# Rotary tables of a two-layer decoder: 16 rows built with frequency and token group on the partitions, instead of 128 rows built by transposes

## The chip, the cores and the metric

The program runs on one core of a Trainium2 chip. The metric is the device time of one execution in microseconds, as the median of repeated runs. The core's engines work side by side, each in its own instruction order: TensorE (PE; its weight loads are shown apart as PEld), VectorE (DVE), ScalarE (ACT), GpSimd (POOL) and SyncE (SP, which here only issues transfers). Transfers are issued on the queues of SP, ACT and POOL.

## The reference, cut to what matters

Two layers follow each other over 1024 tokens of width 1024. A layer norms the stream, multiplies it with one combined weight matrix of 5376 columns, runs a sliding-window attention (8 query heads, 2 key/value heads of 64) and a gated linear recurrence on parts of the product, merges both under gates, and adds an output projection to the stream. All is float32. The change is to the tables of the rotary embedding, which turns the first 16 of the 64 entries of each query and key head:

```python
def partial_rope(x, positions):
    half = ROT_DIM // 2                                   # 8
    inv_freq = jnp.power(ROPE_THETA, -jnp.arange(half, dtype=jnp.float32) * (2.0 / ROT_DIM))
    ang = positions.astype(jnp.float32)[..., None] * inv_freq
    cos = jnp.cos(ang)[:, :, None, :]
    sin = jnp.sin(ang)[:, :, None, :]
    xr = x[..., :ROT_DIM].astype(jnp.float32)
    x1, x2 = xr[..., :half], xr[..., half:]
    rot = jnp.concatenate([x1 * cos - x2 * sin, x2 * cos + x1 * sin], axis=-1)
    return jnp.concatenate([rot.astype(x.dtype), x[..., ROT_DIM:]], axis=-1)

h = rms_norm(x, norm_w[layer])
proj = h @ w_in[layer]
(q, k, v, z_attn, q_h, f_h, i_h, g_h, gate_attn, gate_hgrn) = jnp.split(proj, split_points, axis=-1)
q = partial_rope(q.reshape(B, T, N_HEADS, HEAD_DIM), positions)
k = partial_rope(k.reshape(B, T, N_KV_HEADS, HEAD_DIM), positions)
...
x = x + merged @ w_out[layer]
```

So there are 8 frequencies times 1024 tokens = 8192 angles, and both layers use the same ones.

## The kernel before, in words

**Products.** Every float32 product is made of three matmuls on high and low halves (`hi` rounded, `lo = x - hi`; L394 to L396 in the pairs). The cast that makes `hi` is ScalarE's (L137), the difference `lo` VectorE's (L138).

**Pairs.** The combined projection of a layer is done as 15 pairs of 128-column weight chunks (`pair`, called in a loop over `m`). A pair uses a scheme with seven block products in place of eight: VectorE makes sums of quarter matrices of the weights (`ws`, L379 to L383), ScalarE and VectorE split them, and TensorE accumulates into two PSUM banks, `pb` and `pc` (further names are `th`, `tl` for the split sums of the activations and `hh`, `hl` for the split activations). A pair has 60 matmuls of 128x512, or 84 where the first product, `p1`, was not made ahead (in layer 0 from pair 12 on, in layer 1 from pair 11 on; there ScalarE copies `pb` out at L410 and L435 in place of VectorE's additions at L405, and the bank `pb` is then accumulated into again). Results go through buffers `pq`, an activation on ScalarE and a store.

**The tables.** `constants()` is a generator that the loop over pairs of layer 0 advances by one step behind each pair (two behind the first two). Its first step loads the small constants on SP's queue: `freq` [128, 8], `posi` [128, 8] (L508: token p of block b), sinks and norms. Later steps compute the angles (token on the partition; block and frequency along the row), bring them into the range of the sine and make `sins` and `nrn` (for 1 - 2 sin^2 of the half angle). The last four steps each fill a tile `tab` [128, 4x128] on GpSimd (L577), write the few columns that differ from 1 or 0 on VectorE, turn it by four TensorE transposes (L588) into a PSUM bank `tt`, copy it out on ScalarE (`tabo`, L590) and store it on ScalarE's queue into half of a DRAM table `tabs` [128, 1024] (L591). Table 0 holds cosines (1 in rows that are not turned), table 1 sines (0 there).

**The rotary work.** `rotary()` is a generator that `pair` advances, from pair 9 on (`TURN`), once for each result. GpSimd fills `other` with 0 (L715), loads the two tables into SBUF (`cosT`, `sinT`, L729), and for each of five tiles loads `y` (L719) and four pieces of 8 rows of it, exchanged, into `other` (L724). VectorE multiplies `y` by `cosT` (L734), `other` by `sinT` (L736) and adds them (L737); ScalarE casts the sum to `yh` (L742), VectorE makes the rest (L744), and GpSimd's queue stores both. Later GpSimd loads the turned tiles as `ks` and `qs` (L798), and the attention scores begin (L833).

**What sets the order.** Except for the first tokens, whose order is written by hand, a scheduler in the framework sets the order on each engine from the dependencies, the buffers and costs of its own. So a change at one place can move instructions at others. Each engine then works strictly in its order.

Of the kernel before, what the change touches and what calls it, by code (L numbers as in the profile page):

```python
# [24 lines left out]
HD = 64  # L25
# [16 lines left out]
def trunk_kernel(ctx, tc, x, positions, norm_w, w_in, attn_sinks, hgrn_norm_w, w_up_attn,  # L42
# [444 lines left out]
    tabs = [dp.tile([P, T], F32, name=f"tabs_{i}") for i in range(2)]  # L487
# [3 lines left out]
    def constants():  # L491
# [16 lines left out]
        nc.sync.dma_start(posi, positions.rearrange("o (b p) -> p (o b)", p=P))  # L508
# [35 lines left out]
        posf = cp.tile([P, NB], F32, name="posf")  # L544
        tc.keep_in_program_order(V.tensor_copy(posf, posi))
        ang = cp.tile([P, NB, HALF], F32, name="ang")
# [3 lines left out]
        nrn = cp.tile([P, NB, HALF], F32, name="nrn")  # L550
# [16 lines left out]
        sins = cp.tile([P, NB, HALF], F32, name="sins")  # L567
# [4 lines left out]
        for i in range(2):  # L572
            for g in range(2):
                yield
                b = slice(4 * g, 4 * g + 4)
                t = hp.tile([P, 4, P], F32, tag="po", name=f"tab_{i}_{g}")
                G.memset(t, 1.0 - i)  # L577
                for j in (0, HD):
                    if i:
                        V.tensor_scalar(out=t[:, :, j:j + HALF], in0=sins[:, b], scalar1=-1.0, scalar2=None, op0=ALU.mult)  # L580
                        V.tensor_copy(t[:, :, j + HALF:j + 2 * HALF], sins[:, b])
                    else:
                        for e in (j, j + HALF):
                            V.tensor_scalar(out=t[:, :, e:e + HALF], in0=nrn[:, b], scalar1=-2.0, scalar2=1.0,
                                            op0=ALU.mult, op1=ALU.add)
                tp = bank([P, 4, P], f"tt_{i}_{g}")
                for j in range(4):
                    PE.transpose(tp[:, j], t[:, j], ident)  # L588
# [18 lines left out]
    for L in range(DEPTH):  # L607
# [103 lines left out]
        def rotary():  # L711
            cosT, sinT = (slot([P, T], f"{n}T_{L}") for n in ("cos", "sin"))

# [14 lines left out]
            for t, d in zip((cosT, sinT), tabs):  # L728
                nc.gpsimd.dma_start(t, d)  # L729
# [697 lines left out]
def _constants():  # L1427
    p = np.arange(P)
    side = (p[:, None] <= p[None, :]).astype(np.float32)
    upper = (p[None, :] > p[:, None]).astype(np.int32)  # L1430
    s, t = (p % 32)[:, None], np.arange(32)[None, :]
    diag = (s == t).astype(np.float32)
    lev = [(s // (2 * h) == t // (2 * h)) & (s % (2 * h) < h) & (t % (2 * h) >= h) for h in (1, 2, 4, 8, 16)]
    lev = lev[:1] + [lev[1] & (s % 4 == i) for i in range(2)] + lev[2:4] + [lev[4] & (s // 8 % 2 == i) for i in range(2)]
    lev = np.stack(lev, axis=1).astype(np.int32)
    freq = np.power(np.float32(THETA), -np.arange(HALF, dtype=np.float32) * np.float32(2.0 / 16)).astype(np.float32)
    return {"c_ident": np.eye(P, dtype=np.float32), "c_side": side, "c_upper": upper, "c_diag": diag, "c_lev": lev,
            "c_freq": np.ascontiguousarray(np.broadcast_to(freq, (P, HALF)))}
# [27 lines left out]
```

## Time and profile before

| what | us |
|---|---|
| median of three runs | 1376.55 (1376.39 to 1377.52) |
| the profiled execution | 1377.78 |
| its span in the trace | 1376.0 |
| PE busy in it | 1359.2, x8252 |
| DVE busy | 993.3, x1616 |
| ACT busy | 704.1, x1390 |
| POOL busy | 116.6, x196 |

The span runs from the first to the last event of the profile on the core. Matmuls overlap, so that the duration in a row of TensorE is longer than the distance from one start to the next. In the rows of the timeline the first two columns are the start and the duration in us; behind them stand the engine (SPq and the like are the queues' issues), the line, the operation, what it writes and reads without buffer numbers, and shapes; at the end, in square brackets, how long the engine had been idle and what released it. In the rows of a windows view each engine has its busy us and, in brackets, its number of instructions.

### The profile page before, as it was taken

Reading aid. Unit: us, or ns where it says so; the run is one execution under the profiler, and the core shown is the slowest. Engines: PE = TensorE matmul, PEld = TensorE weight load, DVE = VectorE, ACT = ScalarE, POOL = GpSimd, SP = SyncE. Lnnn points to the kernel's source line nnn. Section 1 sums busy time; section 2 is a strip of 40 time slices with the busy share of each in tenths; the row PEclk is TensorE's granted clock in tenths of the full one; section 3 lists DMA queues with packets and bytes.
Section 4 is the critical chain, followed back from the end, with each engine's and each line's share of the span. In section 5 each row is a group of like instructions: output and inputs, shape, how many; then the busy total and the mean of one; then the engine's idle time right before and its main releaser. Section 6 shows DMA issues by size and latency. Waiting matters only on the chain.

```text
span 1376.0 us, 21533 instructions
## 1 busy us (share of the span) xinstructions
PE 1359.2 (99%) x8252; PEld 1129.6 (82%) x8252; DVE 993.3 (72%) x1616; ACT 704.1 (51%) x1390; POOL 116.6 (8%) x196
## 2 busy tenths in 40 slices
PE   9999999999999999999999999999999999999997
PEld 9888888888877888888888888888887788888885
DVE  5867668843646888599959666777356388867998
ACT  7754334443786665313566333344357766552254
POOL 2000012220000011000000001122100000100000
PEclk9999999999999999999999999999999999999998
DMA  8634477875225742390255345597923476429203
GB/s 274 204 114 145 140 223 212 263 266 208 92 93 190 266 158 78 141 403 38 77 176 188 122 143 178 169 255 223 315 96 100 133 236 207 147 88 404 90 0 123
DMA packets 204375, 240.06 MB, mean 174 GB/s; under 512 B 14288, under 2 KB 140880, under 8 KB 204272
## 3 DMA queue, kind: packets, MB, share of 16 engines
q1 hardware_dynamic: 156528, 145.08, 32.3%
q10 hardware_dynamic: 35088, 52.57, 10.5%
q0 software_dynamic: 12656, 41.04, 9.5%
q8 instruction: 65, 1.06, 0.3%
q14 instruction: 38, 0.31, 0.1%
HBM read 160.00 MB, written 78.64 MB: 173 GB/s over the span
## 4 chain that ended last, share of the span: by engine, by line
PE 89%; DVE 7%; DMA 2%; ACT 2%; issue 1%; DVEq 0%; ACTq 0%; SPq 0%
PE pb L394 6%; PE pb L396 6%; PE pb L395 6%; PE pc L394 4%; PE pc L396 4%; PE pc L395 4%; PE pg L233 3%; PE pg L234 3%; PE pg L235 3%; PE av L893 2%; PE pi L920 2%; PE pi L919 2%; PE pi L921 2%; PE pu_uh L968 2%; PE pj_qh L148 2%; PE pu_uh L970 2%
## 5 line engine op out<-in xcount | busy, mean ns | idle before, releaser
L137 ACT CAST whi_s<-ws 128x1024 fp32r<-128x1024 f32 x30 | 31.6, 1053 | 88.3 <-PE pc L396 88.3
L405 DVE TENSOR_TENSOR pq<-pc,pq 128x512 f32<-128x512 f32 x37 | 25.5, 690 | 61.4 <-PE pc L396 56.3
L631 ACT ACTIVATE pq<-pq 128x512 f32<-128x512 f32 x60 | 37.9, 631 | 44.4 <-DVE pq L405 42.9
L137 ACT CAST whi_o<-wo 128x1024 fp32r<-128x1024 f32 x20 | 21.1, 1054 | 77.0 <-PE pu_uh L970 35.5
L137 ACT CAST whi_t<-ws 128x1024 fp32r<-128x1024 f32 x30 | 31.6, 1055 | 41.9 <-PE pc L396 28.0
L968 PE MATMUL pu_ua<-wh_a,wlo_ua 128*128 128x512 f32 x128 | 52.0, 406 | 0.0
L857 ACT ACTIVATE pr<-pr,mx 128x128 f32<-128x128 f32 x128 | 49.6, 390 | 4.1 <-DVE mx L854 3.7
L1152 POOL COPY scT<-acc 32x256 f32<-32x256 f32 x32 | 26.3, 821 | 288.1 <-DVE acc L1149 169.5
L968 PE MATMUL pu_uh<-wh_b,wlo_uh 128*128 128x512 f32 x128 | 50.1, 391 | 0.5 <-DVE u L976 0.5
L970 PE MATMUL pu_ua<-wh_a,whi_ua 128*128 128x512 f32 x128 | 50.4, 394 | 0.0
L969 PE MATMUL pu_ua<-wl_a,whi_ua 128*128 128x512 f32 x128 | 49.9, 390 | 0.0
L969 PE MATMUL pu_uh<-wl_b,whi_uh 128*128 128x512 f32 x128 | 49.8, 389 | 0.0
L970 PE MATMUL pu_uh<-wh_b,whi_uh 128*128 128x512 f32 x128 | 49.8, 389 | 0.0
L394 PE MATMUL pb<-th,wl 128*128 128x512 f32 x120 | 47.1, 393 | 0.5 <-ACT pq L435 0.4
L394 PE MATMUL pb<-th,wlo_s 128*128 128x512 f32 x120 | 47.2, 394 | 0.2 <-DVE wlo_s L138 0.2
L233 PE MATMUL pg<-hh,wl_p 128*128 128x512 f32 (+1 forms) x128 | 46.9, 366 | 0.3 <-DVE wl_p L470 0.3
L394 PE MATMUL pc<-hh,wlo_t 128*128 128x512 f32 x120 | 46.9, 390 | 0.0
L395 PE MATMUL pb<-tl,whi_s 128*128 128x512 f32 x120 | 46.7, 390 | 0.0
L396 PE MATMUL pb<-th,whi_s 128*128 128x512 f32 x120 | 46.7, 389 | 0.0
L394 PE MATMUL pc<-th,wlo_s 128*128 128x512 f32 x120 | 46.7, 389 | 0.0
L395 PE MATMUL pb<-tl,wh 128*128 128x512 f32 x120 | 46.7, 389 | 0.0
L396 PE MATMUL pb<-th,wh 128*128 128x512 f32 x120 | 46.7, 389 | 0.0
(447 smaller groups left out, 4468.2 us busy)
## 6 DMA issues: line engine op xcount, KB each, us to landing
wr<-in_w_in_dram SPq DMA_DIRECT2D x72, 512.0 KB, 4.6
gd<-pq ACTq DMA_DIRECT2D x79, 256.0 KB, 3.0
fq<-fq ACTq DMA_DIRECT2D x48, 256.0 KB, 2.8
wr_p<-in_w_in_dram SPq DMA_DIRECT2D x23, 512.0 KB, 5.2
x<-in_x_dram SPq DMA_DIRECT2D x16, 512.0 KB, 7.5
qs<-qsd POOLq DMA_DIRECT2D x16, 512.0 KB, 7.6
u<-gd SPq DMA_DIRECT2D x16, 512.0 KB, 10.2
ga<-gd SPq DMA_DIRECT2D x16, 512.0 KB, 10.2
```

The costliest lines, as they stand in the source:

```text
L137: S.copy(hi, raw)
L233: PE.matmul(acc, lhsT=wl[:, k], rhs=h[:, t], start=k == ks[0][0], stop=False, skip_group_check=q > 0)
L234: PE.matmul(acc, lhsT=wh[:, k], rhs=l[:, t], start=False, stop=False, skip_group_check=q > 0)
L235: PE.matmul(acc, lhsT=wh[:, k], rhs=h[:, t], start=False, stop=k == ks[q][3], skip_group_check=q > 0)
L394: PE.matmul(acc, lhsT=wl[:, k], rhs=h, start=start and k == 0, stop=False, skip_group_check=not start)
L395: PE.matmul(acc, lhsT=wh[:, k], rhs=l, start=False, stop=False, skip_group_check=not start)
L396: PE.matmul(acc, lhsT=wh[:, k], rhs=h, start=False, stop=k == 3, skip_group_check=not start)
L631: S.activation(d, src, AF.Sigmoid if r < 2 * KT else AF.Silu)
L857: S.activation(pr[:, h], pr[:, h], AF.Exp, bias=mx[:, h:h + 1], accum_out=sm[:, h:h + 1])
L968: PE.matmul(acc, lhsT=w[1][:, k, c], rhs=hi[:, i], start=k == 0, stop=False)
L969: PE.matmul(acc, lhsT=w[0][:, k, c], rhs=lo[:, i], start=False, stop=False)
L970: PE.matmul(acc, lhsT=w[0][:, k, c], rhs=hi[:, i], start=False, stop=k == 3)
```

## The change

The angles are laid out anew: partition f*16 + g holds frequency f of the 64 tokens of group g, so that all tables are [128, 64] tiles. `posi` is loaded eight times, once for each frequency, into 16 partitions each. `freq` is a column [128, 1], and one operation makes all angles instead of eight. The DRAM tables keep only 2 x 8 rows, [16, 1024]; each is written by two stores of a [128, 64] tile (cosines twice; minus sine and sine). The four `tab` tiles with their fills, VectorE writes, transposes, PSUM banks, copies and stores are gone. `rotary()` now fills `cosT` with 1 and `sinT` with 0 on GpSimd in each layer and loads the 16 rows twice into each, at rows 0 and 64.

```diff
-    tabs = [dp.tile([P, T], F32, name=f"tabs_{i}") for i in range(2)]
+    tabs = [dp.tile([2 * HALF, T], F32, name=f"tabs_{i}") for i in range(2)]
...
-        freq = cp.tile([P, HALF], F32, name="freq")
+        freq = cp.tile([P, 1], F32, name="freq")
         nc.sync.dma_start(freq, c_freq)
-        posi = cp.tile([P, NB], I32, name="posi")
-        nc.sync.dma_start(posi, positions.rearrange("o (b p) -> p (o b)", p=P))
+        rows = P // HALF
+        posi = cp.tile([P, T // rows], I32, name="posi")
+        for f in range(HALF):
+            nc.sync.dma_start(posi[f * rows:(f + 1) * rows], positions.rearrange("o (g e) -> (o g) e", g=rows))
...
-        for b in range(NB):
-            V.tensor_scalar(out=ang[:, b], in0=freq, scalar1=posf[:, b:b + 1], scalar2=None, op0=ALU.mult)
+        V.tensor_scalar(out=ang, in0=posf, scalar1=freq, scalar2=None, op0=ALU.mult)
...
         V.tensor_tensor(out=nrn, in0=nrn, in1=nrn, op=ALU.mult)
-        for i in range(2):
-            for g in range(2):
-                yield
-                b = slice(4 * g, 4 * g + 4)
-                t = hp.tile([P, 4, P], F32, tag="po", name=f"tab_{i}_{g}")
-                G.memset(t, 1.0 - i)
...
-                tp = bank([P, 4, P], f"tt_{i}_{g}")
-                for j in range(4):
-                    PE.transpose(tp[:, j], t[:, j], ident)
-                o = hp.tile([P, 4, P], F32, tag="po", name=f"tabo_{i}_{g}")
-                S.copy(o, tp)
-                nc.scalar.dma_start(tabs[i][:, g * 512:(g + 1) * 512], o.rearrange("p j t -> p (j t)"))
+        V.tensor_scalar(out=nrn, in0=nrn, scalar1=-2.0, scalar2=1.0, op0=ALU.mult, op1=ALU.add)
+        V.tensor_scalar(out=ang, in0=sins, scalar1=-1.0, scalar2=None, op0=ALU.mult)
+        yield
+        for i, halves in enumerate(((nrn, nrn), (ang, sins))):
+            for j, t in enumerate(halves):
+                nc.scalar.dma_start(tabs[i][j * HALF:(j + 1) * HALF].rearrange("f (g e) -> (f g) e", g=rows), t)
...
         def rotary():
             cosT, sinT = (slot([P, T], f"{n}T_{L}") for n in ("cos", "sin"))
+            G.memset(cosT, 1.0)
+            G.memset(sinT, 0.0)
...
             for t, d in zip((cosT, sinT), tabs):
-                nc.gpsimd.dma_start(t, d)
+                for r in (0, HD):
+                    nc.gpsimd.dma_start(t[r:r + 2 * HALF], d)
```

The scheduler's order moves with it. In the rows below, a name ends in the layer, the pair and a buffer number. First TensorE in pair 4 of layer 0, where the first table stood; before:

```order
L394 MATMUL pb_0_4_1495<-th_0_1_0_821,wlo_0_4_s_1482 128x512
L395 MATMUL pb_0_4_1495<-tl_0_1_0_822,whi_0_4_s_1481 128x512
L396 MATMUL pb_0_4_1495<-th_0_1_0_821,whi_0_4_s_1481 128x512
L588 MATMUL tt_0_0_1465<-ident_111,tab_0_0_1459 128x128 x4
L394 MATMUL pb_0_4_1495<-th_0_1_1_942,wlo_0_4_s_1482 128x512
L395 MATMUL pb_0_4_1495<-tl_0_1_1_943,whi_0_4_s_1481 128x512
```

and now:

```order
L394 MATMUL pb_0_4_1487<-th_0_1_0_821,wlo_0_4_s_1474 128x512
L395 MATMUL pb_0_4_1487<-tl_0_1_0_822,whi_0_4_s_1473 128x512
L396 MATMUL pb_0_4_1487<-th_0_1_0_821,whi_0_4_s_1473 128x512
L394 MATMUL pb_0_4_1487<-th_0_1_1_942,wlo_0_4_s_1474 128x512
L395 MATMUL pb_0_4_1487<-tl_0_1_1_943,whi_0_4_s_1473 128x512
```

The four transposes are gone; the matmuls around them follow each other as they did. The same holds in pairs 5, 6 and 7.

Second, TensorE at the end of pair 12 of layer 1, where the bank `pb` of pair 12 is accumulated into again after ScalarE has copied it out, and ScalarE's order around that copy (L435); before:

```order
L396 MATMUL pb_1_12_8384<-th_1_2_1_7018,whi_1_12_t_8376 128x512
L394 MATMUL pb_1_13_8531<-hh_1_0_0_6203,wlo_1_13_a_8512 128x512
L394 MATMUL pb_1_12_8384<-th_1_3_0_6966,wl_1_12_8381 128x512
L395 MATMUL pb_1_12_8384<-tl_1_3_0_6967,wh_1_12_8380 128x512
L396 MATMUL pb_1_12_8384<-th_1_3_0_6966,wh_1_12_8380 128x512
```

```order
L410 COPY pq_1_12_12_8436<-pb_1_12_8384 128x512
L742 CAST yh_1_4_8614<-y_1_4_8418 128x1024
L137 CAST whi_1_13_a_8511<-wr_1_13_0_8505 128x1024
L435 COPY pq_1_12_22_8450<-pb_1_12_8384 128x512
L631 ACTIVATE pq_1_12_22_8450<-pq_1_12_22_8450 128x512
```

and now:

```order
L396 MATMUL pb_1_12_8342<-th_1_2_1_6972,whi_1_12_t_8334 128x512
L394 MATMUL pb_1_13_8489<-hh_1_0_0_6157,wlo_1_13_a_8470 128x512
L395 MATMUL pb_1_13_8489<-hl_1_0_0_6165,whi_1_13_a_8469 128x512
L396 MATMUL pb_1_13_8489<-hh_1_0_0_6157,whi_1_13_a_8469 128x512
L394 MATMUL pb_1_13_8489<-hh_1_0_0_6157,wlo_1_13_a_8470 128x512
L394 MATMUL pb_1_12_8342<-th_1_3_0_6920,wl_1_12_8339 128x512
```

```order
L410 COPY pq_1_12_12_8394<-pb_1_12_8342 128x512
L137 CAST whi_1_13_a_8469<-wr_1_13_0_8463 128x1024
L733 CAST yh_1_4_8572<-y_1_4_8376 128x1024
L435 COPY pq_1_12_22_8408<-pb_1_12_8342 128x512
L619 ACTIVATE pq_1_12_22_8408<-pq_1_12_22_8408 128x512
```

On TensorE three more matmuls of pair 13 stand ahead of the first one that writes `pb` of pair 12 again; on ScalarE the cast of the rotated tile and the cast of the weights have changed places ahead of the copy.

Third, VectorE where the rotary work of layer 0 begins; before:

```order
L405 TENSOR_TENSOR pq_0_8_22_1957<-pb_0_8_1929,pq_0_8_22_1957 128x512
L734 TENSOR_TENSOR y_0_0_2078<-y_0_0_2078,cosT_0_2072 128x1024
L405 TENSOR_TENSOR pq_0_8_12_1943<-pc_0_8_1930,pq_0_8_12_1943 128x512
L138 TENSOR_TENSOR wlo_0_9_t_2020<-ws_0_9_1_2010,whi_0_9_t_2019 128x1024
L405 TENSOR_TENSOR pq_0_8_21_2001<-pb_0_8_1929,p1_0_8_835 128x512
L388 TENSOR_TENSOR wl_0_9_2024<-wr_0_9_1_2007,wh_0_9_2023 128x512
```

and now:

```order
L405 TENSOR_TENSOR pq_0_8_22_1907<-pb_0_8_1879,pq_0_8_22_1907 128x512
L405 TENSOR_TENSOR pq_0_8_12_1893<-pc_0_8_1880,pq_0_8_12_1893 128x512
L138 TENSOR_TENSOR wlo_0_9_t_1970<-ws_0_9_1_1960,whi_0_9_t_1969 128x1024
L405 TENSOR_TENSOR pq_0_8_21_1951<-pb_0_8_1879,p1_0_8_835 128x512
L388 TENSOR_TENSOR wl_0_9_1974<-wr_0_9_1_1957,wh_0_9_1973 128x512
L725 TENSOR_TENSOR y_0_0_2032<-y_0_0_2032,cosT_0_2022 128x1024
```

The first rotary product has moved from between two additions of pair 8 to behind the last weight split of pair 9.

More of the change, by code (lines that the diff above doesn't have):

```diff
@@ L541, in constants @@
         yield
-        posf = cp.tile([P, NB], F32, name="posf")
+        wide = [P, T // rows]
+        posf = cp.tile(wide, F32, name="posf")
         tc.keep_in_program_order(V.tensor_copy(posf, posi))
-        ang = cp.tile([P, NB, HALF], F32, name="ang")
-        for b in range(NB):
-            V.tensor_scalar(out=ang[:, b], in0=freq, scalar1=posf[:, b:b + 1], scalar2=None, op0=ALU.mult)
+        ang = cp.tile(wide, F32, name="ang")
+        V.tensor_scalar(out=ang, in0=posf, scalar1=freq, scalar2=None, op0=ALU.mult)
         yield
-        nrn = cp.tile([P, NB, HALF], F32, name="nrn")
+        nrn = cp.tile(wide, F32, name="nrn")
         big = 1.5 * 2.0 ** 23
@@ L566, in constants @@
         V.tensor_scalar(out=ang, in0=ang, scalar1=3.1415925, scalar2=-3.1415925, op0=ALU.min, op1=ALU.max)
-        sins = cp.tile([P, NB, HALF], F32, name="sins")
+        sins = cp.tile(wide, F32, name="sins")
         S.activation(sins, ang, AF.Sin)
```

10 lines of the change are left out of this document (1 added, 9 removed).

## The prediction, made before the result was known

> **What bounds the kernel now.** I read the page first: busy times, the slices of the granted clock, and the chain of waits.
>
> ```profile
> PE 1359.2 (99%) x8252; PEld 1129.6 (82%) x8252; DVE 993.3 (72%) x1616; ACT 704.1 (51%) x1390; POOL 116.6 (8%) x196
> ...
> PEclk9999999999999999999999999999999999999998
> ...
> PE 89%; DVE 7%; DMA 2%; ACT 2%; issue 1%; DVEq 0%; ACTq 0%; SPq 0%
> ```
>
> TensorE is busy for 99% of the span at full clock, and 89% of the chain is TensorE. A busy share can hide slack, because matmuls overlap, so I next cut the first layer into its pairs of weight chunks (60 matmuls of 128x512 each, numbered from 0; 127.33 begins pair 3) by the windows view. Columns: window, its length, then busy us of PE, PEld, DVE, ACT and POOL with counts, clock, DMA share, GB/s.
>
> ```profile
> 127.33:140.93 13.60, 13.60 (x61) 11.27 (x60) 8.87 (x12) 5.81 (x7) 0.52 (x1) 1.00 0.43 136
> 140.93:155.09 14.16, 14.16 (x66) 11.58 (x64) 9.16 (x16) 5.11 (x7) 0.53 (x1) 1.00 0.49 148
> 155.09:169.24 14.15, 14.15 (x65) 11.58 (x64) 9.16 (x16) 5.12 (x7) 0.53 (x1) 1.00 0.50 150
> 169.24:183.39 14.15, 14.15 (x65) 11.57 (x64) 9.16 (x16) 5.12 (x7) 1.91 (x3) 1.00 0.60 186
> 183.39:197.55 14.16, 14.16 (x66) 11.58 (x64) 9.16 (x16) 5.11 (x7) 3.62 (x7) 1.00 0.80 246
> 197.55:211.15 13.60, 13.60 (x62) 11.27 (x60) 10.01 (x13) 4.52 (x6) 0.00 (x0) 1.00 0.48 160
> 211.15:224.75 13.60, 13.60 (x62) 11.27 (x60) 13.05 (x16) 5.50 (x7) 6.25 (x12) 1.00 0.62 195
> ```
>
> A pair takes 13.60 us, 0.2267 us a matmul, in the last row too, where DVE works 13.05 of 13.60. So TensorE's issue rate sets the pace, and only what it issues, or waits for, counts. The four long pairs are the four with a group of table transposes (64 weight loads instead of 60).
>
> **The change, part by part.**
>
> *The transposes.* 16 of them go, four in each of four pairs. Four windows give 14.16 + 14.15 + 14.15 + 14.16 = 56.62 us; four plain ones are 4 x 13.60 = 54.40. The difference is 2.22 us. The timeline of TensorE around one group agrees:
>
> ```profile
> 142.07 0.39 PE L396 MATMUL pb<-th,whi_s 128*128 128x512 f32 x1
> 142.32 0.63 PE L588 MATMUL tt<-ident,tab 128*128 128x128 f32 x4
> 142.70 0.49 PE L394 MATMUL pb<-th,wlo_s 128*128 128x512 f32 x1
> 143.02 0.40 PE L395 MATMUL pb<-tl,whi_s 128*128 128x512 f32 x1
> ```
>
> From 142.07 to 143.02 is 0.95 us for two steps that cost 0.45 elsewhere: 0.50 lost at once, 2.00 over four groups, the low bound; the rest of the 0.555 a pair is in the slightly longer steps behind it. I take 2.22, since the windows hold both. The Trainium skill (TensorE: Matmul & The Clock Gate, Back-to-back issue gap) gives some 81 ns for each 128-wide matmul with its weight load in a stream. By that the 16 would be an estimated 1.30 us, and the whole sum below would be 0.92 us smaller; here the windows disagree with it, at 139 ns each.
>
> *The order at the end of layer 1's pair 12.* The new program puts four matmuls of the next pair, not one, ahead of the matmuls that accumulate again into bank pb. TensorE loses time there now; the second group is the same place in layer 0, where four already stand ahead:
>
> ```profile
> 941.74 0.39 PE L396 MATMUL pb<-th,whi_t 128*128 128x512 f32 x1
> 941.97 0.40 PE L394 MATMUL pb<-hh,wlo_a 128*128 128x512 f32 x1
> 942.81 0.50 PE L394 MATMUL pb<-th,wl 128*128 128x512 f32 x1 [0.44 <-ACT pq L435]
> 943.14 0.40 PE L395 MATMUL pb<-tl,wh 128*128 128x512 f32 x1
> ...
> 266.25 0.39 PE L394 MATMUL pb<-hh,wlo_a 128*128 128x512 f32 x1
> 266.48 0.43 PE L394 MATMUL pb<-th,wl 128*128 128x512 f32 x1
> 266.75 0.40 PE L395 MATMUL pb<-tl,wh 128*128 128x512 f32 x1
> ```
>
> Layer 1: 943.14 - 941.97 = 1.17 for two steps of 0.45 together, 0.72 lost. Layer 0: 266.75 - 266.25 = 0.50, 0.05 lost. What TensorE waits for is ScalarE's copy out of pb (L435):
>
> ```profile
> 938.09 1.05 ACT L742 CAST yh<-y 128x1024 fp32r<-128x1024 f32 x1 [0.78 <-DVE y L737]
> 939.45 1.06 ACT L137 CAST whi_a<-wr 128x1024 fp32r<-128x1024 f32 x1 [0.30 <-PE pc L396]
> 942.17 0.58 ACT L435 COPY pq<-pb 128x512 f32<-128x512 f32 x1 [1.67 <-PE pb L396]
> ```
>
> The copy ends at 942.75; four matmuls of 0.2267 from 941.97 end at 942.88, so the wait is covered: gain 0.67. Bounds: 0 if the copy comes late, 0.72 if all of it goes. The new ScalarE order puts the cast of the rotated tile (yh) directly ahead of that copy: from 939.45 + 1.06 = 940.51 to 941.56, 0.6 us before the copy can start. VectorE's sum that it waits for now has that 0.6 us more, and no more.
>
> *The rotary work on VectorE* (L734 to L744, five tiles in each layer) keeps its 20 operations a layer, but the first stands after pair 9's first wl instead of inside pair 8.
>
> ```profile
> 206.51 1.22 DVE L734 TENSOR_TENSOR y<-y,cosT 128x1024 f32<-128x1024 f32 x1
> ...
> 282.01 1.23 DVE L744 TENSOR_TENSOR y<-y,yh 128x1024 fp32r<-128x1024 f32 x1 [1.11 <-ACT yh L742]
> ```
>
> The 20 come to four for each of the pairs 9 to 13, about what the window 211.15:224.75 carries, where TensorE lost nothing. In the program's order the fullest pair of layer 0 has six, now as before, but one with five follows it where three did. I take 0; with the cover gone, the price of one such operation ahead of a bank's evacuation is at most its 1.22 us. The small table operations on VectorE and the four PSUM copies on ScalarE lie in pairs where VectorE is busy 9.16 of 14.16 and ScalarE 5.11: worth 0 on the path.
>
> *POOL and the tables' way.* Two fills and four small loads replace four fills and two large loads. The tables are now stored among the results of pair 2, whose window ends at 127.33; before, the last store lay in the window that starts at 183.39.
>
> ```profile
> 176.51 0.53 POOL L577 MEMSET tab<- 128x512 f32 x1 [13.48 <-ACT whi_s L137]
> 176.98 0.95 POOL L715 MEMSET other<- 128x1024 f32 x1
> 177.88 0.54 POOL L729 DMA_DIRECT2D cosT<-tabs  x1
> 191.09 0.55 POOL L729 DMA_DIRECT2D sinT<-tabs  x1 [12.67 <-DMA tabs<-tabo]
> ...
> 297.29 1.75 POOL L798 DMA_DIRECT2D qs<-qsd  x3 [4.63 <-PE pb L396]
> ...
> 324.12 0.33 PE L833 MATMUL sc<-ks,qs 128*128 128x128 f32 x2
> ```
>
> What is queued behind the tables' loads on POOL is the rotary input. POOL waited 12.67 us for the old stores; added work is two fills of 0.95 less four of 0.53, and two issues of 0.54: below 1 us a layer. At the other end POOL waits 4.63 us for TensorE before it loads qs, and the scores begin 26 us later, so even a late rotary end moves nothing: 0.
>
> *The start.* Seven more loads of positions stand on SP's queue ahead of the gate weights.
>
> ```profile
> 28.88 0.43 SPq L508 DMA_DIRECT2D posi<-in_positions_dram  x1
> 29.36 0.58 SPq L510 DMA_DIRECT2D sink<-in_attn_sinks_dram  x1
> 30.16 0.38 SPq L512 DMA_DIRECT2D hnw<-in_hgrn_norm_w_dram  x1
> 30.74 1.70 SPq L514 DMA_DIRECT2D lbl<-in_lb_logits_dram  x1
> 34.92 0.37 SPq L94 DMA_DIRECT2D wr_p<-in_w_in_dram  x1
> ...
> 36.14 0.37 SPq L94 DMA_DIRECT2D wr_p<-in_w_in_dram  x1
> ...
> wr_p<-in_w_in_dram SPq DMA_DIRECT2D x23, 512.0 KB, 5.2
> ...
> 41.39 1.06 ACT L137 CAST whi_p<-wr_p 128x1024 fp32r<-128x1024 f32 x1 [2.38 <-DMA wr_p<-in_w_in_dram]
> ```
>
> 7 x 0.48 (28.88 to 29.36) is 3.4 us; SP was free from 32.44 to 34.92, 2.5 us. So the first weight load is up to 0.9 us late and the second up to 0.1 (35.8 + 0.48 against 36.14). ScalarE waits 2.38 us for a weight load, until 41.39. With the usual 5.2 us to landing that is the second (36.14 + 5.2 = 41.3), not the first (40.1). So I take 0, with bounds of 0 and 0.9. The Trainium skill (DMA: Bandwidth & Descriptors, Rules for kernel authors) says that transfers under 64 KB are mostly overhead and should be coalesced, which speaks against eight loads of 4 KB; by it the cost would be queue time like that just counted, and no run here shows it yet.
>
> **The sum.** -2.22 - 0.67 = -2.89. The profiled execution took 1377.78 (span 1376.0, 1.78 around it), which becomes 1374.9 with a span of 1373.1. That execution lies 1.23 above the median of the runs, so the median 1376.55 becomes **1373.7**. A difference of 0.2%, 2.75 us, is about the least that a measurement of this kernel can tell from no change, down to 1373.8: the forecast lies on that edge.
>
> **The rivals.**
>
> *Only the transposes count.* The yh cast waits for VectorE longer than its 0.6 us margin, the copy stays late, or the lost 0.7 us turns up in another pair, since the scheduler reshuffled ten of them. For it: VectorE is full there; against: the margin of 0.6 us, and layer 0 with the same order of matmuls. Time 1376.55 - 2.22 = 1374.3.
>
> *The start pays.* ScalarE's late load is passed on in full: 1373.7 + 0.9 = 1374.6. For it: a real wait of 2.38 us ending at 41.39; against: the load waited for is late by 0.1 at most if each issue takes 0.48.
>
> *A transpose costs less than its window.* If only the extra weight loads' time in the windows goes (11.58 - 11.27 = 0.31 a pair, 1.24 for four) and the rest of the 0.555 stays as pace: -1.24 - 0.67, 1374.6. Against it: the pairs before and behind run at 13.60. By the 81 ns that the Trainium skill gives (the section named above) the time would be an estimated 1376.55 - 1.30 - 0.67 = 1374.6, the same.
>
> *The squeezed rotary work becomes the bound.* VectorE works in order; a rotary operation that stands ahead of the read of a bank makes TensorE wait, as the copy at 942 did. At that price, 0.72 us, it decides from five stalls on (3.6 against 2.89); one in each of pairs 9 to 13 of both layers is ten, 7.2: 1376.55 - 2.89 + 7.2 = 1380.9, slower. For it: 13.05 of 13.60 busy, and less room on the left; against: full pairs already run at 13.60.
>
> **How the numbers follow.** Forecast 0.62 (its own range 1373.1 to 1374.3), transposes only 0.17, the start 0.06, cheap transposes 0.06, rotary bound 0.09. Of the forecast I put some two thirds below 1373.8 (0.42) and of the small rivals 0.02: faster 0.44. Slower by over 0.2% is most of the last rival, 0.07; the rest of it loses less than it must. That leaves 0.49 within 0.2%. The range runs from 1372.8 (one more stall of 0.72 gone, and the 0.16 by which the lowest run lies under the median) to 1376.0 (1376.55 less the 1.24 of the weight loads, plus one new stall of 0.72), which takes in the three small rivals; the bound rotary case is left out.
>
> **What would show it.** Pairs 4 to 7 of layer 0 take 13.60 us like the others (if over 13.7, the first term fails). At the end of layer 1's pair 12 TensorE has no gap over 0.3 us between starts, and yh ends before the copy starts. Windows of pairs 9 to 13 stay at 13.60 in both layers; a longer one names the rotary rival. ScalarE's cast at 41.39 moves by less than 0.3 us; more shows the start rival. The scores of layer 0 begin 2.2 us earlier, near 321.9. It would be wrong as a whole if the gain were under 1 us with those windows at 13.60: then some later stage took it back.

## The result and the profile after

The changed kernel takes 1382.86 us (median of six runs, 1380.38 to 1387.7) against 1376.2 for the kernel before in the same runs: a ratio of 1.0052, interval 1.0038 to 1.0065. It is slower by half a per cent, where 1373.7 was forecast. The profiled execution took 1387.70 with a span of 1385.7. Three executions (1942, 3181 and 5932 us) that were far slower than all the others of the same program are left out of the medians, ranges and ratios below. First the page of the changed kernel: busy times, and the chain of waits.

```profile
PE 1361.0 (98%) x8236; PEld 1130.0 (82%) x8236; DVE 992.4 (72%) x1595; ACT 702.6 (51%) x1386; POOL 119.7 (9%) x200
...
PE 81%; DVE 9%; DMA 6%; ACT 2%; issue 1%; SPq 1%; DVEq 0%; ACTq 0%
```

VectorE and ScalarE are busy a little less than before (993.3 and 704.1 us there), GpSimd 3.1 us more, and TensorE 1.8 us more with 16 instructions fewer. DMA holds 6% of the chain where it held 2%, so something on the path now waits for transfers. The view of TensorE's waits names it:

```profile
PE pb L394 <- DVE pq L405: 3.0, 1, 3.0
PE po L1184 <- DVE R L1171: 2.9, 5, 1.0
PE pb L394 <- DVE wlo_t L138: 2.5, 1, 2.5
```

The first and third of these are new (the columns are total, times, longest); they are single stalls, the first in layer 0 and the other in layer 1. The windows of the pairs of layer 0 (window, length, busy us of PE, PEld, DVE, ACT, POOL with counts, clock, DMA share, GB/s) show where the first one is:

```profile
141.25:154.85 13.60, 13.60 (x61) 11.26 (x60) 9.06 (x12) 4.52 (x6) 0.00 (x0) 1.00 0.42 135
...
182.05:195.65 13.60, 13.60 (x61) 11.26 (x60) 8.88 (x12) 4.52 (x6) 3.15 (x6) 1.00 0.71 222
...
222.85:236.45 13.60, 13.60 (x61) 11.26 (x60) 13.30 (x17) 4.83 (x7) 5.67 (x11) 1.00 0.99 280
236.45:250.36 13.91, 10.89 (x37) 8.45 (x36) 7.37 (x11) 4.63 (x5) 3.35 (x7) 0.78 0.76 233
```

Pairs 4 to 7 take 13.60 us, as the first term of the prediction said. Pair 10, with VectorE busy for 13.30 of 13.60, still takes 13.60. Pair 11 begins with the last row, which has only 36 weight loads in 13.91 us, at a mean clock of 0.78. TensorE there:

```profile
241.67 0.39 PE L396 MATMUL pc<-th,whi_s 128*128 128x512 f32 x1
245.07 0.80 PE L394 MATMUL pb<-th,wlo_t 128*128 128x512 f32 x1 [3.02 <-DVE pq L405]
245.67 0.63 PE L395 MATMUL pb<-tl,whi_t 128*128 128x512 f32 x1
246.09 0.63 PE L396 MATMUL pb<-th,whi_t 128*128 128x512 f32 x1
```

From 241.67 to 245.07 is 3.40 us for a step of 0.227. Then the steps are 0.43 us: TensorE runs at half clock, as the windows of the same stretch show with 0.50:

```profile
245.00:250.50 5.50, 5.43 (x13) 0.50 0.53 117
250.50:256.00 5.50, 5.50 (x25) 0.94 0.86 266
```

VectorE, whose read of the bank (L405) released TensorE, shows why that read was late:

```profile
237.31 0.69 DVE L388 TENSOR_TENSOR wl<-wr,wh 128x512 fp32r<-128x512 f32 x1
243.72 0.69 DVE L379 TENSOR_TENSOR ws<-wr 128x512 f32<-128x512 f32 x1 [5.72 <-DMA wr<-in_w_in_dram]
244.34 0.68 DVE L405 TENSOR_TENSOR pq<-pb,p 128x512 f32<-128x512 f32 x1
```

The sum of weights for pair 12 (L379) waits 5.72 us for a weight load, and the read of bank `pb` stands behind it in VectorE's order. Before the change the same sum waited 0.68 us (its row stands further down). The load in question, on SP's queue, after and before (the second row of each is the time to its landing):

```profile
233.67 0.37 SPq L94 DMA_DIRECT2D wr<-in_w_in_dram  x1
DMA to landing us min/median/max: 10.0/10.0/10.0
```

```profile
229.32 0.85 SPq L94 DMA_DIRECT2D wr<-in_w_in_dram  x1
DMA to landing us min/median/max: 12.1/12.1/12.1
```

It is issued 4.35 us later by the clock of the trace, while TensorE, without the transposes, begins pair 11 1.9 us earlier (236.45 against 238.35). What SP waits for is the buffer: the weight chunks have three, and the load takes over the one whose last reader is VectorE's s4 = a12 - s2 (L383) of pair 11. VectorE after the change, and then before it:

```profile
221.30 0.69 DVE L383 TENSOR_TENSOR ws<-wr,ws 128x512 f32<-128x512 f32 x1
...
230.02 1.22 DVE L727 TENSOR_TENSOR other<-other,sinT 128x1024 f32<-128x1024 f32 x1
...
231.82 1.22 DVE L138 TENSOR_TENSOR wlo_s<-ws,whi_s 128x1024 fp32r<-128x1024 f32 x1
232.96 0.68 DVE L383 TENSOR_TENSOR ws<-wr,ws 128x512 f32<-128x512 f32 x1
```

```profile
215.55 1.21 DVE L737 TENSOR_TENSOR y<-y,other 128x1024 f32<-128x1024 f32 x1
...
217.89 0.68 DVE L383 TENSOR_TENSOR ws<-wr,ws 128x512 f32<-128x512 f32 x1
...
220.22 1.21 DVE L138 TENSOR_TENSOR wlo_s<-ws,whi_s 128x1024 fp32r<-128x1024 f32 x1
...
228.62 0.68 DVE L383 TENSOR_TENSOR ws<-wr,ws 128x512 f32<-128x512 f32 x1
229.22 1.22 DVE L736 TENSOR_TENSOR other<-other,sinT 128x1024 f32<-128x1024 f32 x1
...
232.13 1.22 DVE L138 TENSOR_TENSOR wlo_s<-ws,whi_s 128x1024 fp32r<-128x1024 f32 x1
```

In pair 11 (228.62 before, 232.96 after) s4 stood ahead of the rotary product and of the split `wlo_s`; now it stands behind both. In pair 10 (217.89 and 221.30) a rotary product and the rotary sum stood ahead of it before as well, and only the split is new there.

The load does not meet the rotary stores alone. The eight stores of the key tile are issued from 221.91 to 226.59 and land from 226.4 to 238.1; the weight load ahead of it on SP's queue, issued at 225.51 among them, takes 14.2 us and lands at 239.71, and the load of 233.67 lands 4.0 us behind that, at 243.70.

In layer 1 the sum waits 5.9 us and TensorE stalls for 2.5, but more by a slow landing than by a late issue. The load is issued 3.8 us before pair 11 begins (910.57 against 914.34), where it was 5.0 before the change (904.23 against 909.21); it takes 11.2 us to land instead of 7.4.

The starts of the same TensorE instruction in the two profiled executions, after less before, give the account (worked out from the traces, in us):

| place | difference there | step |
|---|---|---|
| pair 3 of layer 0 | +0.32 | start-up, already +0.40 at 24 us, ahead of the positions' loads |
| pair 11 begins | -1.89 | -2.21: the transposes |
| behind the stall and the half clock | +4.24 | +6.13: 3.18 of stall, 2.95 of half clock |
| end of layer 0 | +5.15 | +0.91: small waits |
| behind the stall in layer 1 | +7.89 | +2.74 |
| behind layer 1's pair 12 | +7.24 | -0.65 |
| last matmul | +9.59 | +2.35: two waits of `po` for `R` in the recurrence (0.40 and 1.01 of idle time) and the steps around them |

### The profile page after: what moved, and what is told of

Same layout as the page of the kernel before. It is cut to its first block, busy times and chain, and to the rows that moved or that the text cites. A ratio compares the mean times of both kernels' runs of the same rounds, so it can differ in the third digit from the quotient of the medians.

```text
span 1385.7 us, 21476 instructions
## 1 busy us (share of the span) xinstructions
PE 1361.0 (98%) x8236; PEld 1130.0 (82%) x8236; DVE 992.4 (72%) x1595; ACT 702.6 (51%) x1386; POOL 119.7 (9%) x200
## 4 chain that ended last, share of the span: by engine, by line
PE 81%; DVE 9%; DMA 6%; ACT 2%; issue 1%; SPq 1%; DVEq 0%; ACTq 0%
PE pb L394 6%; PE pb L395 6%; PE pb L396 6%; PE pc L394 4%; PE pc L395 4%; PE pc L396 4%; PE pg L233 3%; PE pg L235 3%; PE pg L234 3%; PE pi L911 2%; PE pi L910 2%; PE pi L912 2%; PE av L884 2%; PE pu_uh L959 2%; PE pu_uh L960 2%; PE pu_uh L961 2%
## 5 line engine op out<-in xcount | busy, mean ns | idle before, releaser
L405 DVE TENSOR_TENSOR pq<-pc,pq 128x512 f32<-128x512 f32 x37 | 25.5, 690 | 58.2 <-PE pc L396 54.2
L394 PE MATMUL pb<-th,wlo_t 128*128 128x512 f32 x120 | 47.9, 399 | 5.5 <-DVE pq L405 3.0
L396 PE MATMUL pb<-th,whi_t 128*128 128x512 f32 x120 | 47.7, 397 | 0.0
L395 PE MATMUL pb<-tl,whi_t 128*128 128x512 f32 x120 | 47.6, 397 | 0.0
L395 PE MATMUL pc<-hl,whi_t 128*128 128x512 f32 x120 | 46.9, 391 | 0.0
```

Source lines behind the costliest of these rows:

```text
L394: PE.matmul(acc, lhsT=wl[:, k], rhs=h, start=start and k == 0, stop=False, skip_group_check=not start)
L395: PE.matmul(acc, lhsT=wh[:, k], rhs=l, start=False, stop=False, skip_group_check=not start)
L396: PE.matmul(acc, lhsT=wh[:, k], rhs=h, start=False, stop=k == 3, skip_group_check=not start)
```

## The experiments

Theory: the weight load is issued late (s4 moved), lands late (behind the rotary stores), and VectorE's order puts the read of a bank behind the sum that waits for it. Rivals: the new tables' own way (fills, loads, stores, start), the squeezed rotary work itself, or weights that TensorE lacks. "Before" in the ratios is the kernel before, timed beside each.

**The changed kernel again.**

> The changed kernel again, for a second trace of it. Late-weights theory: VectorE's subtraction that frees a weight buffer (s4 = a12 - s2) now stands behind rotary operations in pairs 10 and 11, so the weight load that takes the buffer is issued late (233.67 us in the first trace, 2.8 us before pair 11 begins at 236.45; before the change 9.0 us ahead, 229.32 against 238.35), lands behind the rotary stores, and VectorE's first sum of pair 12 waits 5.7 us for it, with the read of a PSUM bank queued behind it. It expects the same two waits of VectorE for a weight load here (over 4 us in layer 0 near 240 and in layer 1 near 918) and a TensorE stall of 2 to 3.5 us in each. Clock theory: the time varies from 1380.4 to 1387.7 because a TensorE stall of about 3 us costs 2.6 us more of half clock; if this profiled execution is near 1381 no stretch at 0.50 follows the stalls, if it is near 1387 one does. Rival (start, stores or tables cost the time): the gaps near 241 and 925 are absent or below 1 us and the loss lies elsewhere.

1383.15 us, ratio 1.0045 (1.0033 to 1.0058); the profiled execution took 1380.48. Both stalls are there again:

```profile
PE pb L394 <- DVE pq L405: 3.7, 1, 3.7
PE pb L394 <- DVE wlo_t L138: 1.4, 1, 1.4
```

The sizes differ: 3.7 and 1.4 instead of 3.0 and 2.5. The expectation that an execution near 1381 would show no half clock was wrong: seven slow steps follow the stall of 3.7, and the stretch behind it loses 1.7 us, against twelve slow steps and 2.95 us behind the one of 3.0. The loss in the recurrence (2.35 us above) is absent here, so the slowdown does not need it.

**Four weight buffers.** So that a load need not wait for s4, which stays where the changed kernel has it. The other two places that use these buffers get four as well.

```diff
-NSLOT = 39
+NSLOT = 38
...
-wp.tile([P, k, P], F32, tag="wraw", name=f"wr_{nm}", bufs=3)
+wp.tile([P, k, P], F32, tag="wraw", name=f"wr_{nm}", bufs=4)
...
```

> The changed kernel with four buffers instead of three for the weight chunks (and 38 slots instead of 39, for the room). VectorE's order in pairs 8 to 13 stays the same; a load no longer waits for the late subtraction of the chunk three loads back. Late-weights theory: the loads of pair 12 are issued some 8 us or more earlier, VectorE does not wait for them, no TensorE gap over 1 us near 241 and 925, time 1373 to 1375 (before 1376.2 less the 2.2 of the transposes and the 0.7 of the stall in layer 1's pair 12). Rival (the rotary stores hold up whatever load runs beside them): the loads still land late, VectorE still waits over 3 us, time 1380 to 1387. Rival (the squeezed rotary work itself fills VectorE): VectorE does not wait for loads but TensorE still stalls 2 to 3 us in both layers, 1379 to 1384.

1378.9 us, ratio 1.0019 (1.0009 to 1.0028). No TensorE stall near 241 or 925 is left. VectorE's wait did not vanish, as had been expected; it shrank from 5.72 to 2.51 us in layer 0, and from 5.89 to 1.46 in layer 1:

```profile
239.85 0.69 DVE L379 TENSOR_TENSOR ws<-wr 128x512 f32<-128x512 f32 x1 [2.51 <-DMA wr<-in_w_in_dram]
```

The load that the sum of layer 0 waits for is now issued at 224.85, 10.9 us before pair 11 begins instead of 2.8, and still needs 14.9 us to land beside the stores. So the late issue and the slow landing both have a part. The time is 4 us above the expectation; other waits came, in the attention and the recurrence. Whether they come from the slot given up is asked further down.

**s4 held back in the kernel before.**

```diff
...
+            if nm[2:] in ("10", "11"):
+                order.enter_context(tc.issue_after(lowers[-1]))
             V.tensor_tensor(out=s4, in0=a12, in1=s2, op=ALU.subtract)
```

(`lowers[-1]` is the split `wlo_s` of the same pair.)

> The kernel before the change, transposes and tables as they were, with one thing moved: in pairs 10 and 11 of both layers VectorE's subtraction s4 (the last reader of a weight buffer) is queued behind the split wlo_s of the same pair, where the change has it. TensorE's, ScalarE's, GpSimd's and SyncE's orders are unchanged. Late-weights theory: the load of pair 12's second chunk is issued 3 to 5 us later, VectorE waits 3 to 6 us for it, TensorE stalls 2 to 3.5 us in layer 0, layer 1 or both: 1378.5 to 1387. Rival (the tables' new way or the moved rotary work, not the freed buffer): 1376 to 1377, no new TensorE gap over 1 us.

Four runs took 1390.9 to 1402.0 us, ratio 1.0179 (1.0162 to 1.0197), all above the expected range. Nothing but VectorE's order changed, with the old tables and the transposes in place, so the tables' new way is not needed for the loss. Here the first stall is 10.4 us long, and it is not the same load that comes late: the last two experiments take the pairs apart.

**The waiting sum behind the reads.** The loads stay late; only what stands behind the sum changes.

```diff
...
+            if nm[2:] == "12":
+                order.enter_context(tc.issue_after(reads[-1]))
             V.tensor_tensor(out=s1, in0=a21, in1=a22, op=ALU.add)
...
```

(`reads[-1]` is the second read of `pb` in pair 11, or `wlo_t` where pair 11 has no first product made ahead.)

> The changed kernel with VectorE's first sum of pair 12 (the one that waits for the late load) queued behind the second read of bank pb of pair 11 in layer 0, and behind the split wlo_t of pair 11 in layer 1; all other engines' orders are unchanged, and the loads stay as late as they are. Queue theory (the stall comes from what stands behind the waiting sum, not from weights that TensorE lacks): VectorE still waits for the load, but the two TensorE gaps of 3.4 and 2.9 us go or fall below 1 us each, time 1373.5 to 1376. Rival (TensorE lacks pair 12's weights themselves): the gaps move to the start of pair 12 with 2 us or more each, time 1379 to 1387.

1374.81 us, ratio 0.9988 (0.9979 to 0.9996). The load is as late as ever (issued at 233.89, landed at 242.58 with TensorE's pair 11 from 236.09), and both stalls are gone. VectorE's order in the stretch (L411 is now the read of a bank, L383 the waiting sum):

```profile
241.73 0.69 DVE L411 TENSOR_TENSOR pq<-pc,p 128x512 f32<-128x512 f32 x1 [0.89 <-PE pc L402]
...
244.61 0.68 DVE L411 TENSOR_TENSOR pq<-pb,pq 128x512 f32<-128x512 f32 x1
245.21 0.68 DVE L383 TENSOR_TENSOR ws<-wr 128x512 f32<-128x512 f32 x1
```

The sum now finds its load landed, and the banks are read in time. All of the rotary work is still there, so VectorE's fuller pairs are not the cause by themselves. TensorE did not lack pair 12's weights; what it lacked was the read that stood behind the sum. Against the expectation, VectorE's waits for weight loads are also small (0.9 us at most), because work now fills that time.

**The transposes alone.** The kernel before without them; ScalarE copies the unturned tile, so the tables hold wrong entries.

```diff
-                tp = bank([P, 4, P], f"tt_{i}_{g}")
-                for j in range(4):
-                    PE.transpose(tp[:, j], t[:, j], ident)
...
-                S.copy(o, tp)
+                S.copy(o, t)
```

> The kernel before with the 16 table transposes left out and nothing else (ScalarE copies the unturned tile, so the tables hold the wrong entries); the orders of the engines and the rotary work stay as before. The first term of the sum expects pairs 4 to 7 of layer 0 at 13.60 us each and 2.2 us off the time: 1374.0 to 1374.6. Rival (a transpose costs less than its window): 1375.0 to 1375.8. Late-weights theory: no wait of VectorE for a weight load over 2 us, as before. The stall of 0.7 us at the end of layer 1's pair 12 is expected to stay, since the order there is that of before.

1374.63 us, ratio 0.9989 (0.9980 to 0.9998), and pairs 4 to 7 take 13.60 us each (139.99 to 207.99 for pairs 4 to 8). VectorE's rotary order does not move in this kernel, so it is not the missing transposes that moved it.

**The rotary set-up a pair earlier.**

```diff
             nxt = load(0)
+            yield
             for n, j in enumerate(tiles):
...
+            if m == TURN - 1:
+                next(turning)
             pair(wi, (c0, c1), parts, hT, f"{L}_{m}", p1s[m] if m < ahead else None, use)
```

> The changed kernel with the rotary set-up (fills, loads of the tables and of the first tile) written one pair earlier, ahead of pair 8, and the five tiles' steps where they were. The scheduler then puts VectorE's s4 of pairs 10 to 12 directly behind its other three sums, ahead of the rotary operations, as before the change. Late-weights theory: weight loads of pair 12 are issued before pair 11 begins, VectorE waits under 2 us for any, no TensorE gap over 1 us near 241 and 925, time 1373 to 1375. Rival (the new tables' fills, loads or stores cost the time): 1379 to 1384 as for the changed kernel.

1375.52 us, ratio 0.9991 (0.9982 to 1.0000); half a us above the expected range, but with the stalls gone and the new tables whole. The profiled execution took 1373.80. So the fills, loads and stores of the new tables are not what costs the time.

**38 slots.** The kernel with the waiting sum behind the reads, with one slot fewer.

```diff
-NSLOT = 39
+NSLOT = 38
```

> The kernel of the run that queued the waiting sum behind the reads of the banks (1374.8), with 38 slots in place of 39 and nothing else. If the run with four weight buffers lost its missing 4 us to the slot that it gave up, this one takes 1377 to 1380, with small gaps of TensorE of 0.6 to 0.9 us near 348, 362, 576, 680, 1024, 1038 and 1168 us. If it lost them to the weight loads that start earlier, this one stays at 1374 to 1375.5 without those gaps.

1378.0 us, ratio 1.0009 (1.0000 to 1.0018): 3.2 us above the 39 slots. The slot explains most of what the kernel with four weight buffers lost against the one with 39 slots. About 1 us of its 4.1 stays unexplained.

**The key tile last.** The first tile turned is then a query tile with four stores instead of eight, and the loads of pair 12 are issued as late as in the changed kernel.

```diff
-            tiles = (0, 1, 2, 4, 5)
+            tiles = (1, 2, 4, 5, 0)
...
```

> The changed kernel with the key tile (eight stores of 256 KB) turned last instead of first; the first tile is now a query tile with four stores. VectorE's order in pairs 9 to 11 stays the changed one, so the weight loads of pair 12 are issued as late as before (2 to 3 us before pair 11 begins). Collision part of the late-weights theory: the loads that ran beside the eight stores took 14 and 10 us instead of 4.7; with half the bytes they land some 3 to 5 us sooner, VectorE waits 0 to 3 us, and the stall in layer 0 falls below 1.5 us with no half clock behind it: 1374.5 to 1378.5. Rival (the late issue alone, whatever runs beside it): waits of 5 to 6 us as in the changed kernel, 1380 to 1387.

1374.45 us, ratio 0.9987 (0.9978 to 0.9996). The load, on SP's queue with its time to landing:

```profile
233.96 0.37 SPq L94 DMA_DIRECT2D wr<-in_w_in_dram  x1
DMA to landing us min/median/max: 4.9/4.9/4.9
```

It is issued 2.8 us before pair 11 begins (236.72), exactly as in the changed kernel, but lands in 4.9 us instead of 10.0, and the sum finds it landed. The four stores had all landed by 231.3, and the weight load ahead of it on the queue landed at 235.62 instead of 239.71; the load in question follows it by 3.2 us, where it was 4.0. So the late issue alone does no harm; it needs the eight stores ahead of it. This version has the lowest median of all and beats both kernels, but the next two (1374.81 and 1374.99) are not told apart from it.

**Both mends.** The key tile last and the set-up early.

```diff
-            tiles = (0, 1, 2, 4, 5)
+            tiles = (1, 2, 4, 5, 0)
...
+            if m == TURN - 1:
+                next(turning)
...
```

> The changed kernel with both mends that need no more room: the key tile turned last, and the rotary set-up written one pair earlier. The loads of pair 12 are then issued before pair 11 begins and beside half the stores. Late-weights theory: no wait of VectorE for a weight load over 1 us; the gains of the change come through whole, 1373 to 1374.5, with a narrower spread than the run with the early set-up alone (1373.8 to 1378.1). Rival (the early set-up itself costs something at times, the spread of that run): median above 1375.

1374.99 us, ratio 0.9988 (0.9980 to 0.9997), half a us above the range and no better than the key tile last alone.

**The key tile last, and the waiting sum behind the reads.**

```diff
-            tiles = (0, 1, 2, 4, 5)
+            tiles = (1, 2, 4, 5, 0)
...
+            if nm[2:] == "12":
+                order.enter_context(tc.issue_after(reads[-1]))
...
```

> The changed kernel with the key tile last and the first sum of pair 12 queued behind the reads of the banks. If the loads in the run with the key tile last already land in time (it took 1374.45), the second mend adds nothing: 1374 to 1375. If some of its runs still lose to a late load, this one is lower and narrower: 1373 to 1374.

1376.5 us, ratio 1.0002 (0.9993 to 1.0011): the expectation missed by 1.5 us. The second mend costs 2 us where there is nothing to mend. TensorE loses 0.6 us at 264 and 0.9 us at 284, at the ends of pairs 12 and 13 of layer 0, counted instruction by instruction against the kernel with the key tile last, which has no wait there; for this one added constraint the scheduler moved rows on TensorE and ScalarE too. The longer wait:

```profile
283.94 0.50 PE L400 MATMUL pb<-th,wl 128*128 128x512 f32 x1 [0.68 <-ACT pq L441]
```

As with the change itself, a constraint at one place moved rows at others. The other 0.5 us was not traced.

**s4 held back in pair 11 alone.** As above, with `"11"` only.

> The kernel before the change with s4 queued behind the split wlo_s in pair 11 alone (the run with pairs 10 and 11 took 1400). Late-weights theory: the load of pair 12's second chunk waits for this s4 of pair 11, so it is issued 3 to 4 us later than before; the load of pair 11's second chunk, which waits for pair 10's, is not. That is about as late against pair 11's start as in the changed kernel less one step: VectorE waits 2 to 6 us, TensorE stalls 0 to 3.5 us a layer, 1377 to 1385, well below 1400. Clock theory: a stall in which TensorE has nothing left to do for less than about 2.6 us is followed by full clock, one of 3.0 us or more by some 2 us or more of half clock. Rival (pair 10's s4 alone did it): 1376 to 1377.

1376.72 us, ratio 1.0001 (0.9992 to 1.0010): the rival was right. The load was issued at 233.06, nearly as late as in the changed kernel, but landed in 6.6 us, and pair 11 began only at 237.96. VectorE did wait 2.3 us for a load in layer 1, the low end of what was expected, but TensorE did not stall. So a late s4 in pair 11 is not enough by itself.

**s4 held back in pair 10 alone.** With `"10"` only.

> The kernel before the change with s4 queued behind the split wlo_s in pair 10 alone; pair 11 as before. The run with both pairs took 1400, with pair 11 alone 1376.7. First-link theory: the harm begins in pair 10: its s4 frees the buffer for pair 11's second chunk, whose load is then issued near 221.2 instead of 218.6 us, some 2 us behind the first of the eight key stores (218.8) instead of just ahead of them, and lands near 238 instead of 223; VectorE's first sum of pair 11 waits 8 us or more, TensorE stalls 5 us or more in layer 0: 1385 to 1402, about as with both. Rival (both pairs are needed): 1376 to 1380, VectorE waits under 3 us. Clock theory as before: half clock behind a TensorE idle time of 3.0 us or more, none behind 2.6 us or less.

1391.9 us, ratio 1.0100 (1.0083 to 1.0117). The load of pair 11's second chunk, issued at 221.5, and the sum that waits for it:

```profile
DMA to landing us min/median/max: 16.9/16.9/16.9
...
238.44 0.69 DVE L381 TENSOR_TENSOR ws<-wr 128x512 f32<-128x512 f32 x1 [12.08 <-DMA wr<-in_w_in_dram]
```

```profile
240.99 0.79 PE L398 MATMUL pb<-th,wlo_t 128*128 128x512 f32 x1 [10.58 <-DVE pq L409]
241.58 0.63 PE L399 MATMUL pb<-tl,whi_t 128*128 128x512 f32 x1
242.01 0.63 PE L400 MATMUL pb<-th,whi_t 128*128 128x512 f32 x1
```

In the kernel before the same load was issued at 218.60 and landed in 4.6 us. Issued 2.9 us later, behind five of the eight key stores (219.09 to 221.24), it took 16.9. The loss in this kernel begins in pair 10, as expected. In the changed kernel it does not: there that load was issued at 222.02, behind one of the stores, and landed in 5.6 us, and the one that came too late was pair 12's, issued at 233.67. So the two runs that hold back pair 10's s4 show that a late s4 can stall TensorE in this way, but not by the load that stalls the changed kernel.

## Why the prediction was wrong, point by point

- **The transposes: right.** Forecast 2.22, found 2.21 in the changed kernel and 13.60 us in each of the four pairs.
- **The order at the end of layer 1's pair 12: right.** Forecast 0.67, found 0.65. The copy is covered as described: four matmuls of pair 13 run ahead, the cast of `yh` ends before the copy starts.

```profile
949.84 0.39 PE L394 MATMUL pb<-hh,wlo_a 128*128 128x512 f32 x1
...
950.75 0.43 PE L394 MATMUL pb<-th,wl 128*128 128x512 f32 x1
951.02 0.40 PE L395 MATMUL pb<-tl,wh 128*128 128x512 f32 x1
```

```profile
948.28 1.05 ACT L733 CAST yh<-y 128x1024 fp32r<-128x1024 f32 x1
950.04 0.59 ACT L435 COPY pq<-pb 128x512 f32<-128x512 f32 x1 [0.71 <-PE pb L396]
```

- **The rotary work on VectorE, "I take 0": the step that failed.** It counted the operations in each pair and asked only whether a rotary operation stands ahead of the read of a bank, at 1.22 us at most. It did not ask what the rows that moved set free. The rows that matter are the four sums of the next pair's weights. The last of them frees a weight buffer; behind it hang SP's load, that load's landing behind the rotary stores, the next sum, and the read of a bank behind that sum. What the prediction put at 0 cost two stalls of 3.0 and 2.5 us in the profiled execution, with 2.95 us of half clock behind the first. The runs bear out the links in the changed kernel: with the sum behind the reads the stalls are gone (1374.81), with half the stores ahead of the load they are gone (1374.45), and with a fourth buffer, so that the load need not wait for s4, they are gone too, though that kernel loses time elsewhere (1378.9). A late s4 in pair 11 alone did no harm in the kernel before (1376.72), where the stores came earlier and pair 11 later.
- **POOL and the tables' way, and the start: right at 0, in part by luck.** The kernel with the set-up earlier keeps all of the new tables' transfers and takes 1375.5. POOL's added work, "below 1 us a layer", holds for layer 0 alone: in layer 1 two fills and two issues come and nothing goes. The eight loads of positions took 5.69 us, 0.71 each and not 0.48; the weight load behind them moved by only 0.44 us (34.92 to 35.36) because the small loads started 0.8 us earlier and the one of `lbl` took 0.47 instead of 1.70. By its own sign the start rival would have shown: ScalarE's cast at 41.39 moved to 42.08, 0.69, where 0.3 was the limit. But 0.40 of that is a lag that TensorE has at 24 us, before the first load of positions, and it does not grow over that stretch (+0.32 in pair 3).
- **The rivals.** "The squeezed rotary work becomes the bound", at 0.09, had the right engine, the right sign and nearly the time (1380.9), but another mechanism: ten stalls of 0.72 spread over five pairs, where there are two (3.0 and 2.5 us, and 3.7 and 1.4 in the second trace), and a row waiting for a load instead of rotary work ahead of a read. The sign that the prediction named for it, a window of pairs 9 to 13 longer than 13.60, came true in pair 11, but would have led to the wrong mechanism: pair 10, the fullest, stays at 13.60. That the order could delay a transfer was no rival at all.
- **The clock.** The prediction priced a stall at its length. In the profiled execution the stall in layer 0 cost nearly twice that, 6.13 for 3.18.
- **The range.** It ended at 1376.0 because it allowed for one new stall of 0.72 us, the price of the wait for the copy at 942. What it should have allowed for was a late load. In the trace of before, the load behind the rotary stores already took 12.1 us to its landing, and VectorE already waited 0.68 us for it: there was no margin, and that was there to be read. VectorE before:

```profile
241.48 0.69 DVE L379 TENSOR_TENSOR ws<-wr 128x512 f32<-128x512 f32 x1 [0.68 <-DMA wr<-in_w_in_dram]
```

So the change's own gain is real and was given back: 2.21 and 0.65 us in the trace, and by the medians 0.9 to 2.0 us in the kernels with the new tables, all 39 slots and neither the two stalls nor new ones (1374.45 to 1375.52). Why the medians show less than the trace was not followed.

What stays open: how much of the lateness belongs to the issue (4.35 us), to TensorE's lead without transposes (1.9) and to the stores, which begin 3 us later. Counted from the start of pair 11 of layer 0 in each trace, the load that the first sum of pair 12 waits for landed 3.0 us behind it in the kernel before, 7.3 in the changed kernel, 4.0 with four buffers, 2.1 with the key tile last, and 1.7 in the kernel before with s4 held back in pair 11 alone. So an earlier issue or half the stores is enough, and so are the earlier stores and later pair 11 of the kernel before, but the shares add up in no simple way and were not measured apart. In layer 1 the issue is only 1.2 us later by that count, and the landing takes 3.8 us longer. Nor was it tried which of the fills and loads of the tables made the scheduler move the rows.

## What to carry to other kernels

When a change lets a scheduler move rows, follow each moved row forward through what it frees, a buffer above all, to the transfer that waits for the buffer and the first reader of that transfer, and compare the time left with the landing time that the trace shows beside the same neighbours, not with the median. An instruction that may wait for a transfer should not stand ahead of the read of a PSUM bank in an engine that works in order. A gain on the busiest engine also shortens every margin that other engines had.

## What the runs showed of the hardware

- **A stall of 3 us or more cost more than its length.** Behind idle times of 2.52, 1.68, 1.64 and 1.44 us TensorE went on at full clock; behind 3.02, 3.67, 10.38 and 10.58 us it ran at half clock (0.427 us a step instead of 0.227) for 12, 7, 5 and 9 steps. The Trainium skill (TensorE: Matmul & The Clock Gate, Why this matters for your kernels) says to leave no idle gap over some 3 us between bursts of matmuls; these rows agree. The Trainium skill (TensorE: Matmul & The Clock Gate, Part 1: The HAM clock gate) also remarks, of the slow matmuls at a kernel's start, that their number varies from run to run; here the number behind a stall varies too, and the longest idle times are not followed by the most slow steps.
- **A weight load's landing depends on its neighbours by a factor of more than three.** The same 512 KB took 4.6 us just ahead of the key tile's eight stores and 16.9 when issued 2.9 us later, behind five of them. At the place where it took 10.0 us, with three of the eight stores and the weight load ahead of it still under way, it took 4.9 when a query tile's four stores had gone ahead instead and had all landed.
